# Hybrid decoder block on one core: 48 sums of 128x512 in the front moved from VectorE to accumulating DMAs of GpSimd's queue

## The chip, the core and the metric

The kernel runs on one core of a Trainium2 chip, as one launch. The metric is the device time in microseconds (us); several executions are given by their median. PE is the matmul engine (TensorE), DVE is VectorE, ACT is ScalarE, POOL is GpSimd, and SP is the engine whose queue issues nearly all loads and stores. Each engine works through its own instructions in the order in which they stand, and waits on semaphores for the others. A DMA is issued by an engine's queue and moved by 16 DMA engines that all queues share.

## The reference

One decoder layer on 1024 tokens of width 1024, in float32. Cut to what matters here:

```python
h = rmsnorm(x, norm_mix_pre)
q, k, v, gate, u = split(h @ w_in)                     # 4 heads of 128; u is 512 wide
qh, kh = rope(q), rope(k) * 128 ** -0.5                # x1*cos - x2*sin, x1*sin + x2*cos
y_ret = silu(gate) * groupnorm(retention(qh, kh, v))   # chunks of 128 tokens
# state space: 32 groups of 16 channels, 64 complex states each
states = scan(lam_bar, b_bar @ u)                      # s[t] = lam_bar*s[t-1] + bu[t]
y_ssm = glu(gelu(real(c @ states) + d * u))
x = x + rmsnorm(concat(y_ret, y_ssm) @ w_out, norm_mix_post)
x = x + rmsnorm(relu(rmsnorm(x) @ w_ff1) ** 2 @ w_ff2, norm_mlp_post)
```

## The kernel before

Tiles lie with 128 channels on the partitions and 512 tokens (or 128x4) in the free direction. Every large matmul is done as three passes over a high and a low part of its operands, which ACT and DVE make from each loaded tile (helper `split`, lines 133 to 139). The program runs in this order on PE: the projection to u, then gate, query and key projections (tiles pg and pj), the values (v), the gated unit (gl), the output projection (mx), and the two MLP products (f1, f2). The **front** is what stands ahead of mx.

Beside the projections, the front carries two side works on the same engines. One is the rotation of queries and keys: for each of 4 heads, query and key, and two halves of the tokens, `qk_unit` multiplies the projection by cosines (tile ra) and, with its halves exchanged, by sines (rb), and adds the two: 16 sums. The other is the state-space scan, which is cut into 8 **parts** of four channel groups (`ssm_part`, parts 0 to 7). The scan runs over 128 blocks of 8 tokens. A part has these steps:

- two products of small tables with phase factors, W and VV (`outer`: two products and a sum each). W makes, through the matmuls kps and wps, the tables MR and WT; VV is the table that turns states into outputs.
- the matmuls xps, which give 128 inputs of the scan; DVE rotates them by a phase (A = xps\*Fr, B = exchanged halves of xps times Fi, then A = A + B).
- four scans of DVE (line 529, B from A), the rotation back (A, C, then SS = A - C).
- the matmuls yps, which add the contribution of the tokens' own block (UT with MT) and that of the states (SS with VV); ACT takes the result (Y), and it is stored.

So a part has four sums of 128x512: W, VV, A and SS. In 8 parts these are 32, and with the rotation's 16 they are 48. A and SS of a part follow one another: SS needs the scans, the scans need A. The last four yps matmuls of a part are the only readers of SS.

The phase tables Fr and Fi come from tables fa and fb that POOL makes by a chain of small products (lines 312 to 317, then 433 and 434). POOL also clears each part's MR (line 506), and raises small tiles to the power -1/2 for the norms (lines 223 and 644). The norm of the first tokens needs such a power, and its result goes through PE again (nb_x, line 247).

The order on each engine is set when the program is built: a scheduler simulates the program with costs of its own and places each instruction where its operands are ready in that simulation. A change of an operation's engine therefore also moves other instructions.

Of the kernel before, what the change touches and what calls it, by code (L numbers as in the profile page):

```python
# [20 lines left out]
MUL, ADD, SUB = ALU.mult, ALU.add, ALU.subtract  # L21
# [3 lines left out]
P = 128  # L25
# [25 lines left out]
def hybrid_block_kernel(ctx, tc, x, xrow, gain, wu, wv, wqkg, wglu, wout, wff1, wff2, lam, bc, dsk,  # L51
                        rope, dmask, xi, zeta, sgn, edge, out):
    nc = tc.nc
    V, S, GP, TE = nc.vector, nc.scalar, nc.gpsimd, nc.tensor
# [8 lines left out]
    def half(name, dt=F32, shape=(P, 512)):  # L63
        tag = re.sub("[0-9_]+", "", name)
        return u2.tile(list(shape), dt, tag=tag, name=name, bufs=BUFS.get(tag))
# [4 lines left out]
    def mi_ps(name, shape=(P, 512)):  # L70
        return pm.tile(list(shape), F32, tag="mi", name=name)
# [22 lines left out]
    def ring(tag, shape, bufs):  # L94

        if tag not in rings:
            rings[tag] = [[const(f"{tag}{i}", shape) for i in range(bufs)], 0]
        r = rings[tag]
        r[1] += 1
        return r[0][r[1] % bufs]  # L100
# [13 lines left out]
    def load(dst, src, lead=None):  # L114
        r = nc.sync.dma_start(dst, src)
        if lead is not None:
            i = bisect.bisect_right(marks, clock[0] - lead, key=lambda m: m[0]) - 1
            if i >= 0:
                tc.add_manual_dep(r.ins, marks[i][1].name, gate_info, reason="load no earlier")
# [8 lines left out]
    def after_mark(r):  # L128
        if mark[0] is not None:
            tc.add_manual_dep(r.ins, mark[0].name, gate_info, reason="in order")  # L130
        return r

    def split(hi, lo, src, scale=None):
        if scale is None:
            after_mark(S.activation(hi, src, AF.Copy))  # L135
            V.tensor_tensor(lo, src, hi.bitcast(F32), op=SUB)  # L136
        else:
            S.activation(hi, src, AF.Copy, scale=scale)
            V.scalar_tensor_tensor(lo, src, scale, hi.bitcast(F32), op0=MUL, op1=SUB)
# [305 lines left out]
    s3 = (P, 4, P)  # L445
# [4 lines left out]
    def phase_tables(j):  # L450

        gs = slice(4 * j, 4 * j + 4)
        shf = [P, 4, T, 16]

        def lowp(m):
            return m[:, :, gs].rearrange("p a g -> p g a").unsqueeze(2).to_broadcast(shf)

        def highp(m):
            return m[:, :, gs].rearrange("p a g -> p g a").unsqueeze(3).to_broadcast(shf)

        def v4(m):
            return m.rearrange("p g (b a) -> p g b a", a=16)

        even, odd = ([half(f"F{z}{2 * j + i}", shape=s3) for z in "ri"] for i in range(2))
        tr, ti = half(f"ftr{j}", shape=s3), half(f"fti{j}", shape=s3)
        cmul(V, V, v4(even[0]), v4(even[1]), lowp(fa_r), lowp(fa_i), highp(fbr), highp(fbi),
             v4(tr), v4(ti))
        for e, o in zip(even, odd):
            load(o[0:64], e[64:128])
            load(o[64:128], e[64:128])  # L470
            load(e[64:128], e[0:64])
        phases[2 * j], phases[2 * j + 1] = even, odd

    def ssm_part(ei):
        if ei % 2 == 0:
            phase_tables(ei // 2)
        g0 = ei * 4
        gs = slice(g0, g0 + 4)
        UT = half(f"UT{ei}", shape=s3)
        for m in range(T):  # L480
            load(UT[m * GC:(m + 1) * GC],
                 ud[T - 1 - m, ei * 64:(ei + 1) * 64, :].rearrange("(g c) n -> c g n", c=GC))

        def outer(dst, a, lr, b, li, nm):
            tmp = half(f"tmp{nm}{ei}", shape=s4)

            def bx(m):
                return m[:, gs].unsqueeze(2).to_broadcast(list(s4))

            def by(m):  # L490
                return m[:, :, gs].rearrange("p m g -> p g m").unsqueeze(3).to_broadcast(list(s4))

            V.tensor_tensor(dst, bx(a), by(lr), op=MUL)
            V.tensor_tensor(tmp, bx(b), by(li), op=MUL)
            V.tensor_tensor(dst, dst, tmp, op=ADD)

        W = half(f"W{ei}", shape=s4)
        outer(W, a_b, qr, b_b, qi, "w")
        kt = ring("kt", (P, 4, GC), 2)
        kps = mi_ps(f"kps{ei}", (P, 4, GC))  # L500
        for g in range(4):
            TE.matmul(kps[:, g], W[:, g], cs[:, g0 + g], start=True, stop=True)
        S.activation(kt, kps, AF.Copy)
        V.tensor_tensor(kt[0:GC], kt[0:GC], de[0:GC, gs], op=ADD)
        MR = half(f"MR{ei}", shape=(P, T, 4, GC))
        GP.memset(MR, 0.0)
        for t in range(T):
            r0 = (T - 1 - t) * GC
            load(MR[r0:P, t], kt[0:P - r0])
        WT = half(f"WT{ei}", shape=s3)  # L510
        wps = mi_ps(f"wps{ei}", s3)
        for g in range(4):
            TE.transpose(wps[:, g], W[:, g].rearrange("p m c -> p (m c)"), ident)
        S.activation(WT, wps, AF.Copy)
        VV = half(f"VV{ei}", shape=s4)
        outer(VV, a_c, vr, b_c, vi, "v")
        yield
        Fr, Fi = phases.pop(ei)
        A, B = half(f"A{ei}", shape=s3), half(f"B{ei}", shape=s3)
        xps = mi_ps(f"xps{ei}", s3)  # L520
        for g in range(4):
            TE.matmul(xps[:, g], WT[:, g], UT[:, g], start=True, stop=True)
        V.tensor_tensor(A, xps, Fr, op=MUL)
        V.tensor_tensor(B[0:64], xps[64:128], Fi[64:128], op=MUL)
        V.scalar_tensor_tensor(B[64:128], xps[0:64], -1.0, Fi[0:64], op0=MUL, op1=MUL)
        V.tensor_tensor(A, A, B, op=ADD)
        yield
        for g in range(4):
            V.tensor_tensor_scan(B[:, g], rho[:, g0 + g:g0 + g + 1].to_broadcast([P, P]),
                                 A[:, g], 0.0, op0=MUL, op1=ADD)  # L530
        n1 = P - 1
        V.tensor_tensor(A[:, :, 0:n1], B[:, :, 0:n1], Fr[:, :, 0:n1], op=MUL)
        C = half(f"C{ei}", shape=s3)
        V.tensor_tensor(C[0:64, :, 0:n1], B[64:128, :, 0:n1], Fi[64:128, :, 0:n1], op=MUL)
        V.scalar_tensor_tensor(C[64:128, :, 0:n1], B[0:64, :, 0:n1], -1.0, Fi[0:64, :, 0:n1],
                               op0=MUL, op1=MUL)
        SS = half(f"SS{ei}", shape=s3)
        V.memset(SS[:, :, 0], 0.0)
        V.tensor_tensor(SS[:, :, 1:P], A[:, :, 0:n1], C[:, :, 0:n1], op=SUB)
        MT = half(f"MT{ei}", shape=s4)  # L540
        S.activation(MT.rearrange("p g t c -> p t g c"), MR, AF.Copy)
        yps = mi_ps(f"yps{ei}", s3)
        for g in range(4):
            TE.matmul(yps[:, g], MT[:, g], UT[:, g], start=True, stop=False)
            TE.matmul(yps[:, g], VV[:, g], SS[:, g], start=False, stop=True)
        Y = half(f"Y{ei}", shape=s3)
        S.activation(Y, yps, AF.Gelu_apprx_tanh)
        load(yd[:, :, gs, :].rearrange("t c g n -> (t c) g n"), Y)
        yield

    def ssm():
        parts = [ssm_part(ei) for ei in range(8)]
        yield next(parts[0])
        for ei in range(8):
            if ei < 7:
                yield next(parts[ei + 1])
            yield from parts[ei]
# [42 lines left out]
    def proj(name, w, hf):  # L600
        ps = acc_ps(name)
        for k in range(KB):
            mm3(ps, wblk(w, k), hT[k][hf], k == 0, k == KB - 1)
        return ps
# [57 lines left out]
    def tick():  # L662
        ticks[0] += 1
        step(1)
        pstep(1)
# [13 lines left out]
    def qk_unit(h, j, w):  # L679
        pair = []  # L680
        for hf in range(2):
            nm = f"{h}{j}{hf}"
            tick()
            ps = proj(f"pj{nm}", w, hf)
            a, b = half(f"ra{nm}", shape=s3), half(f"rb{nm}")
            af = a.rearrange("p c i -> p (c i)")
            V.tensor_tensor(af, ps, tabs[0][hf], op=MUL)
            S.activation(b[0:64], ps[64:128], AF.Copy)
            S.activation(b[64:128], ps[0:64], AF.Copy)
            V.tensor_tensor(b, b, tabs[1][hf], op=MUL)  # L690
            V.tensor_tensor(af, af, b, op=ADD)
            pair.append(a)
        qkv[h, j] = pair

# [131 lines left out]
    def comb(a, b, op, name=None):  # L826

        o = a if name is None else half(name)
        after_mark(V.tensor_tensor(o, a, b, op=op))  # L829
        return o  # L830
# [205 lines left out]
    for i in range(NP):  # L1036
# [3 lines left out]
        s3 = comb(a11, a21, SUB)  # L1040
# [100 lines left out]
    for i in range(NP):  # L1141
# [5 lines left out]
        else:  # L1147
            for b in range(4):
                a, t = ins[i]
# [4 lines left out]
    for c0 in (0, 256):  # L1154
        cols = slice(c0, c0 + 256)
        for b in range(4):
            around(b)
            if c0:
                for i in range(NP - NL, NP):
                    a, t = ins[i]  # L1160
# [103 lines left out]
```

## Time and profile before

| | |
|---|---|
| median of 3 runs | 1077.44 us (1076.61 to 1077.88) |
| the profiled execution, its own time | 1077.59 us |
| its span, first to last instruction | 1075.5 us |
| outside the span | 2.1 us |
| PE busy | 1049.9 us of the span (98%) |
| DVE busy | 770.1 us (72%) |
| ACT busy | 492.6 us (46%) |
| POOL busy | 68.8 us (6%) |
| mean granted clock of PE | 0.992 of full speed |

The profile is of one execution. The span is what the trace covers; the time of the execution is longer by 2.1 us. Times in the rows count from the span's start. Busy time of PE is the time in which some matmul is in flight, and matmuls overlap.

### The profile page before, as it was taken

The page shows a single profiled execution, that of the slowest core. Times are in us where ns is not written, and L with a number is a line of the kernel's source. Part 1 is how long each engine was busy: PE and PEld are TensorE (multiplying, and loading weights), DVE is VectorE, ACT ScalarE, POOL GpSimd, SP SyncE. Part 2 cuts the span into 40 slices and gives each one's busy share as a digit, 9 for nine tenths or more (in the row PEclk, how much of TensorE's full clock was granted, in tenths as well). Part 3 has the DMA queues.
Part 4 walks back from the last instruction along what each step waited for, and adds up shares of the span by engine and source line. Part 5 has one row for each costly group of instructions (what it writes and reads, how often), then busy time and mean ns, then how long its engine had stood idle before and what let it go on. Part 6 is the DMA issues. An engine that isn't in the chain of part 4 may idle for free.

```text
span 1075.5 us, 15286 instructions
## 1 busy us (share of the span) xinstructions
PE 1049.9 (98%) x5248; PEld 891.5 (83%) x5248; DVE 770.1 (72%) x1446; ACT 492.6 (46%) x916; POOL 68.8 (6%) x101
## 2 busy tenths in 40 slices
PE   7998999999999999999999999999999999999995
PEld 6877889989988888788888888888888888888895
DVE  7887999568766107478888888886763885756965
ACT  7332334355555224466644444464732553525712
POOL 0240000001000122300000000000000000000002
PEclk9998999999999999999999999999999999999998
DMA  9644343221431105386366666656982565579324
GB/s 317 205 125 114 98 123 96 74 79 36 133 103 58 41 1 200 115 309 229 126 228 234 231 237 224 214 183 218 375 276 85 181 203 175 187 229 328 127 85 150
DMA packets 126285, 181.58 MB, mean 169 GB/s; under 512 B 35584, under 2 KB 43776, under 8 KB 126208
## 3 DMA queue, kind: packets, MB, share of 16 engines
q1 hardware_dynamic: 125664, 180.09, 50.9%
q8 instruction: 41, 0.67, 0.2%
q10 hardware_dynamic: 544, 0.52, 0.1%
q14 instruction: 36, 0.29, 0.1%
HBM read 130.62 MB, written 45.61 MB: 164 GB/s over the span
## 4 chain that ended last, share of the span: by engine, by line
PE 79%; DVE 2%; issue 1%; DMA 1%; POOL 1%; ACT 1%; DVEq 0%; SPq 0%; ACTq 0%; POOLq 0%
PE f2x L106 15%; PE f2y L106 12%; PE f1z L106 8%; PE f1y L106 8%; PE mx L106 8%; PE f1x L106 8%; PE pj L106 4%; PE gl L106 4%; PE f1w L106 4%; PE v L106 3%; PE y L636 1%; PE st L611 1%; DMA raw_wo<-wout_dram 1%; PE y L638 1%; PE sps L622 1%
## 5 line engine op out<-in xcount | busy, mean ns | idle before, releaser
L106 PE MATMUL f2x<-hi_tc,lo_sb 128*128 128x512 f32 x216 | 84.0, 389 | 0.0
L106 PE MATMUL f2x<-lo_tc,hi_sb 128*128 128x512 f32 x216 | 84.0, 389 | 0.0
L106 PE MATMUL f2x<-hi_tc,hi_sb 128*128 128x512 f32 x216 | 83.7, 390 | 0.0
L135 ACT ACTIVATE hi_sa<-rawa 128x512 fp32r<-128x512 f32 x80 | 48.3, 622 | 59.2 <-DVE rawa L829 57.0
L106 PE MATMUL f2y<-hi_tc,hi_sb 128*128 128x512 f32 x192 | 74.7, 389 | 0.0
L106 PE MATMUL f2y<-lo_tc,hi_sb 128*128 128x512 f32 x192 | 74.7, 389 | 0.0
L106 PE MATMUL f2y<-hi_tc,lo_sb 128*128 128x512 f32 x192 | 74.7, 389 | 0.0
L136 DVE TENSOR_TENSOR lo_sa<-rawa,hi_sa 128x512 fp32r<-128x512 f32 x80 | 56.3, 710 | 8.9 <-ACT hi_sa L135 8.9
L223 POOL TENSOR_TENSOR small<-small 128x4 f32<-128x4 f32 (+1 forms) x9 | 10.1, 1119 | 653.1 <-DVE small L221 653.1
L106 PE MATMUL pj<-hi_h,hi_wqkg 128*128 128x512 f32 x128 | 50.8, 397 | 0.0
L106 PE MATMUL pj<-lo_h,hi_wqkg 128*128 128x512 f32 x128 | 50.7, 396 | 0.0
L106 PE MATMUL pj<-hi_h,lo_wqkg 128*128 128x512 f32 x128 | 50.5, 395 | 0.0
L106 PE MATMUL f1x<-lo_tb,hi_sa 128*128 128x512 f32 x128 | 49.9, 390 | 0.4 <-DVE lo_tb L136 0.4
L106 PE MATMUL f1x<-hi_tb,hi_sa 128*128 128x512 f32 x128 | 50.1, 392 | 0.0
L106 PE MATMUL f1y<-hi_tb,hi_sa 128*128 128x512 f32 x128 | 49.8, 389 | 0.0
L106 PE MATMUL f1y<-lo_tb,hi_sa 128*128 128x512 f32 x128 | 49.8, 389 | 0.0
L106 PE MATMUL f1y<-hi_tb,lo_sa 128*128 128x512 f32 x128 | 49.8, 389 | 0.0
L106 PE MATMUL f1z<-hi_tb,hi_sa 128*128 128x512 f32 x128 | 49.8, 389 | 0.0
L106 PE MATMUL f1z<-lo_tb,hi_sa 128*128 128x512 f32 x128 | 49.8, 389 | 0.0
L106 PE MATMUL f1z<-hi_tb,lo_sa 128*128 128x512 f32 x128 | 49.8, 389 | 0.0
L106 PE MATMUL f1x<-hi_tb,lo_sa 128*128 128x512 f32 x128 | 49.3, 390 | 0.0
L106 PEld LDWEIGHTS f2x<-lo_tc,hi_sb 128*128 128x128 f32 x216 | 40.6, 188 | 8.4
(398 smaller groups left out, 2998.9 us busy)
## 6 DMA issues: line engine op xcount, KB each, us to landing
rawa<-wff_dram SPq DMA_DIRECT2D x92, 256.0 KB, 3.3
tinx<-td SPq DMA_DIRECT2D x48, 256.0 KB, 3.9
tiny<-td SPq DMA_DIRECT2D x48, 256.0 KB, 3.4
raw_wqkg<-wqkg_dram SPq DMA_DIRECT2D x24, 256.0 KB, 2.9
x<-x_dram SPq DMA_DIRECT2D x16, 256.0 KB, 5.4
xt<-xrow_dram SPq DMA_DIRECT2D x16, 256.0 KB, 3.7
raw_wo<-wout_dram SPq DMA_DIRECT2D x16, 256.0 KB, 3.4
xr<-x_dram SPq DMA_DIRECT2D x16, 256.0 KB, 3.4
```

Source lines behind the costliest of these rows:

```text
L106: r = TE.matmul(out_, lhsT, rhs, **kw)
L135: after_mark(S.activation(hi, src, AF.Copy))
L136: V.tensor_tensor(lo, src, hi.bitcast(F32), op=SUB)
L223: GP.tensor_tensor(r, t, mhalf[:, 0:n], op=ALU.pow)
L611: TE.matmul(stp[:, i], k_[:, i], q_[:, i], start=True, stop=True)
L622: TE.matmul(sps[:, i], kz[:, i], v_[:, i], start=True, stop=True)
L636: TE.matmul(yps[:, i], smk[:, i], v_[:, i], start=True, stop=(c == 0))
L638: TE.matmul(yps[:, i], q_[:, i], Rs[(c - 1) // 4][:, (c - 1) % 4], start=False, stop=True)
```

## The change

A new helper issues an accumulating DMA from GpSimd's queue: it reads the source tile and the destination tile, and writes their sum to the destination. All 48 sums named above go through it. For SS, whose second term was subtracted, the signs of C's two products are exchanged, and the products are written at their shifted place at once, with the first column of both tiles cleared; so the sum can cover the whole tile. That adds one DVE memset for each part. The new lines shift the line numbers behind them by 4: line 529 is line 533 after the change.

```diff
+    def dma_add(o, a):
+
+        GP.dma_start(o, a, accum_op=ADD)
+
...
             V.tensor_tensor(dst, bx(a), by(lr), op=MUL)
             V.tensor_tensor(tmp, bx(b), by(li), op=MUL)
-            V.tensor_tensor(dst, dst, tmp, op=ADD)
+            dma_add(dst, tmp)
...
         V.scalar_tensor_tensor(B[64:128], xps[0:64], -1.0, Fi[0:64], op0=MUL, op1=MUL)
-        V.tensor_tensor(A, A, B, op=ADD)
+        dma_add(A, B)
         yield
...
         n1 = P - 1
-        V.tensor_tensor(A[:, :, 0:n1], B[:, :, 0:n1], Fr[:, :, 0:n1], op=MUL)
-        C = half(f"C{ei}", shape=s3)
-        V.tensor_tensor(C[0:64, :, 0:n1], B[64:128, :, 0:n1], Fi[64:128, :, 0:n1], op=MUL)
-        V.scalar_tensor_tensor(C[64:128, :, 0:n1], B[0:64, :, 0:n1], -1.0, Fi[0:64, :, 0:n1],
+        SS, C = half(f"SS{ei}", shape=s3), half(f"C{ei}", shape=s3)
+        V.memset(SS[:, :, 0], 0.0)
+        V.memset(C[:, :, 0], 0.0)
+        V.tensor_tensor(SS[:, :, 1:P], B[:, :, 0:n1], Fr[:, :, 0:n1], op=MUL)
+        V.scalar_tensor_tensor(C[0:64, :, 1:P], B[64:128, :, 0:n1], -1.0, Fi[64:128, :, 0:n1],
                                op0=MUL, op1=MUL)
-        SS = half(f"SS{ei}", shape=s3)
-        V.memset(SS[:, :, 0], 0.0)
-        V.tensor_tensor(SS[:, :, 1:P], A[:, :, 0:n1], C[:, :, 0:n1], op=SUB)
+        V.tensor_tensor(C[64:128, :, 1:P], B[0:64, :, 0:n1], Fi[0:64, :, 0:n1], op=MUL)
+        dma_add(SS, C)
...
             V.tensor_tensor(b, b, tabs[1][hf], op=MUL)
-            V.tensor_tensor(af, af, b, op=ADD)
+            dma_add(af, b)
```

The order of instructions on three engines, at the places that the prediction speaks of. The digit behind a tile's name is the part, and the number behind it is the buffer's.

DVE, from the rotation of part 0's scan inputs to its SS. Before:

```order
L526 TENSOR_TENSOR A0_952<-A0_952,B0_953 128x512
L673 TENSOR_TENSOR ga30_1254<-pg30_1229,R0_398 128x512
L529 SCALAR_TENSOR_TENSOR B0_953<-small_72,A0_952 128x128 x4
L675 SCALAR_TENSOR_TENSOR ga30_1254<-gb30_1255,ga30_1254 128x512
L532 TENSOR_TENSOR A0_952<-B0_953,Fr0_776 128x4x127
L534 TENSOR_TENSOR C0_998<-B0_953,Fi0_777 64x4x127
L535 SCALAR_TENSOR_TENSOR C0_998<-B0_953,Fi0_777 64x4x127
L136 TENSOR_TENSOR lo_wqkg1_0_1335<-raw_wqkg1_0_1332,hi_wqkg1_0_1334 128x512
L493 TENSOR_TENSOR W3_1268<-bc0_276,qw_608 128x512
L539 TENSOR_TENSOR SS0_1001<-A0_952,C0_998 128x4x127
```

After:

```order
L529 SCALAR_TENSOR_TENSOR B0_953<-xps0_954,Fi0_777 64x512
L508 TENSOR_TENSOR small_72<-small_72,de_732 16x64
L677 TENSOR_TENSOR ga30_1256<-pg30_1231,R0_398 128x512
L533 SCALAR_TENSOR_TENSOR B0_953<-small_72,A0_952 128x128 x4
L679 SCALAR_TENSOR_TENSOR ga30_1256<-gb30_1257,ga30_1256 128x512
L539 TENSOR_TENSOR SS0_997<-B0_953,Fr0_776 128x4x127
L540 SCALAR_TENSOR_TENSOR C0_998<-B0_953,Fi0_777 64x4x127
L542 TENSOR_TENSOR C0_998<-B0_953,Fi0_777 64x4x127
```

The two sums are gone from DVE. The scans now wait for the DMA of A, and between B and the scans stand two other instructions, a short one and one of 128x512.

POOL, from the end of the chain for fb to the power that the second half's norm needs. Before:

```order
L314 TENSOR_TENSOR fb_668<-fb_668,t8_610 128x16
L317 TENSOR_TENSOR fb_668<-fb_668,t8_610 128x16
L506 MEMSET MR2_1099 128x512
L223 TENSOR_TENSOR small_72<-small_72 128x4
L506 MEMSET MR3_1280 128x512
```

After:

```order
L318 TENSOR_TENSOR fb_668<-fb_668,t8_610 128x16
L321 TENSOR_TENSOR fb_668<-fb_668,t8_610 128x16
L510 MEMSET MR2_1100 128x512
L135 DMA W2_1088<-tmpw2_1089 128x512
L227 TENSOR_TENSOR small_72<-small_72 128x4
L135 DMA A0_952<-B0_953 128x512
L135 DMA SS0_997<-C0_998 128x512
L135 DMA W3_1270<-tmpw3_1271 128x512
L135 DMA A1_1152<-B1_1153 128x512
L510 MEMSET MR3_1282 128x512
L135 DMA VV2_1117<-tmpv2_1118 128x512
L135 DMA SS1_1209<-C1_1210 128x512
```

The DMAs of all parts stand in one queue with the memsets and the powers. Ahead of this piece, three DMAs (VV0, W0, VV1) stand in front of the chain for fa and one (W1) inside the chain for fb.

PE, where the xps matmuls of part 4 stand. Before:

```order
L106 MATMUL pj110_1759<-hi_h70_174,hi_wqkg4_1_1600 128x512
L522 MATMUL xps4_1750<-UT4_1474,WT4_1505 128x128 x4
L106 MATMUL pj110_1759<-lo_h70_175,hi_wqkg4_1_1600 128x512
L106 MATMUL pj110_1759<-hi_h70_174,lo_wqkg4_1_1601 128x512
L106 MATMUL pj111_1816<-hi_h01_204,hi_wqkg4_0_1594 128x512
```

After:

```order
L548 MATMUL yps3_1621<-UT3_1261,MT3_1619 128x128
L549 MATMUL yps3_1621<-SS3_1611,VV3_1299 128x128
L526 MATMUL xps4_1754<-UT4_1477,WT4_1508 128x128 x4
L106 MATMUL pj110_1763<-hi_h00_84,hi_wqkg4_0_1597 128x512
L106 MATMUL pj110_1763<-lo_h00_85,hi_wqkg4_0_1597 128x512
```

Before, the xps matmuls of part 4 stood ahead of the yps matmuls of part 3 that read SS; after, they stand right behind them. Counted over the whole front, the matmuls between the last xps and the first yps that reads SS, for parts 0 to 7, were 60, 78, 87, 111, 136, 69, 108 and 82 before (of 512 columns: 47, 62, 74, 91, 26, 50, 0 and 0), and are 70, 82, 73, 71, 80, 69, 114 and 109 after (of 512 columns: 57, 66, 60, 55, 48, 50, 0 and 0; nearly all others of parts 4, 6 and 7 have 256 columns).

## Rows read from the trace of the kernel before

**Rows 1.** The page, part 1: busy us (share of the span) and instructions of each engine.

```profile
PE 1049.9 (98%) x5248; PEld 891.5 (83%) x5248; DVE 770.1 (72%) x1446; ACT 492.6 (46%) x916; POOL 68.8 (6%) x101
```

**Rows 2.** Idle time of PE by what ended it: us in total, times, longest.

```profile
PE u L106 <- ACT hi_h L138: 5.9, 1, 5.9
PE nb_x L247 <- POOL small L223: 5.8, 1, 5.8
PE yps L545 <- DVE SS L539: 1.4, 1, 1.4
```

**Rows 3.** Three stretches of the front: us, busy time by engine, clock, DMA share, GB/s.

```profile
75.00:100.00 25.00, 19.14 (x77) 15.37 (x76) 19.66 (x32) 7.91 (x14) 2.02 (x1) 0.86 0.43 114
100.00:175.00 75.00, 75.00 (x429) 65.42 (x429) 72.88 (x127) 26.97 (x47) 2.11 (x4) 1.00 0.38 106
175.00:345.00 170.00, 168.49 (x1110) 153.15 (x1109) 121.76 (x278) 82.37 (x165) 11.31 (x9) 1.00 0.28 81
```

**Rows 4.** Timeline, 64 to 87 us: start, duration, instruction, idle time ahead of it.

```profile
64.06 1.06 DVE L312 TENSOR_TENSOR Fr<-fa,fb 128x512 f32<-128x512 f32 x1 [4.12 <-POOL fb L314]
...
82.27 0.15 DVE L221 TENSOR_SCALAR small<-small 128x4 f32<-128x4 f32 x1
...
82.50 2.02 POOL L223 TENSOR_TENSOR small<-small 128x4 f32<-128x4 f32 x1 [14.88 <-DVE small L221]
...
84.57 2.07 PE L247 MATMUL nb_x<-small 128*128 128x128 f32 x8 [5.77 <-POOL small L223]
...
86.87 0.63 PE L106 MATMUL pg<-hi_h,lo_wqkg 128*128 128x512 f32 x1
```

**Rows 5.** DVE's groups, 0 to 320 us: count | busy us, mean ns of one.

```profile
L691 DVE TENSOR_TENSOR ra<-ra,rb 128x512 f32<-128x512 f32 x16 | 11.0, 687 | 0.2
...
L526 DVE TENSOR_TENSOR A<-A,B 128x512 f32<-128x512 f32 x8 | 5.5, 683 | 0.0
```

**Rows 6.** The longest pieces of the chain that ended last, 60 to 345 us: start, us.

```profile
201.22 5.25 PE pj L106 x23
...
281.93 7.66 PE v L106 x64
```

**Rows 7.** Timeline of part 0 (first two), part 4 and part 7 (last four).

```profile
101.87 1.05 PE L522 MATMUL xps<-UT,WT 128*128 128x128 f32 x8
...
102.96 0.69 DVE L523 TENSOR_TENSOR A<-xps,Fr 128x512 f32<-128x512 f32 x1 [1.54 <-PE xps L522]
...
161.31 1.05 PE L522 MATMUL xps<-UT,WT 128*128 128x128 f32 x8
...
168.62 0.67 DVE L523 TENSOR_TENSOR A<-xps,Fr 128x512 f32<-128x512 f32 x1
...
182.95 0.68 DVE L539 TENSOR_TENSOR SS<-A,C 128x508 f32<-128x508 f32 x1
...
183.69 0.49 PE L545 MATMUL yps<-SS,VV 128*128 128x128 f32 x2 [1.37 <-DVE SS L539]
...
278.21 1.06 PE L522 MATMUL xps<-UT,WT 128*128 128x128 f32 x8
...
281.62 0.68 DVE L523 TENSOR_TENSOR A<-xps,Fr 128x512 f32<-128x512 f32 x1
...
288.66 0.69 DVE L539 TENSOR_TENSOR SS<-A,C 128x508 f32<-128x508 f32 x1
...
289.43 0.47 PE L545 MATMUL yps<-SS,VV 128*128 128x128 f32 x2
```

**Rows 8.** DMA issues: count, KB each, median us from issue to landing.

```profile
ud<-uT SPq DMA_DIRECT2D x8, 256.0 KB, 2.6
...
yd<-Y SPq DMA_DIRECT2D x8, 256.0 KB, 2.1
...
MR<-small SPq DMA_DIRECT2D x8, 32.0 KB, 1.9
```

**Rows 9.** POOL's groups: count | busy us, mean ns of one.

```profile
L644 POOL TENSOR_TENSOR small<-small 128x4 f32<-128x4 f32 x8 | 10.8, 1349 | 143.2 <-DVE small L643 143.2
...
L506 POOL MEMSET MR<- 128x512 f32 x8 | 4.2, 527 | 102.3 <-DMA Fi<-Fi 51.3 <-DMA Fr<-Fr 21.3 <-DMA MR<-small 16.9
```

**Rows 10.** POOL's timeline, 57 to 61 us: two products of one size.

```profile
57.63 2.26 POOL L313 TENSOR_TENSOR t<-fb 128x16 f32<-128x16 f32 x1
...
60.04 0.21 POOL L316 TENSOR_TENSOR t<-fb 128x16 f32<-128x16 f32 x1
```

**Rows 11.** Instructions of two lines: count, ns min/median/max, first and last start.

```profile
L691 DVE TENSOR_TENSOR ra<-ra,rb x16: 670/686/698, 130.9 to 272.0; 128x512 f32<-128x512 f32 x16
...
L611 PE MATMUL st<-ra,ra x64: 270/275/275, 197.4 to 322.2; 128*128 128x128 f32 x64
```

## The prediction

> **What bounds the kernel now.** I read the busy times first: PE is busy in 98% of the span, DVE in 72%, POOL in 6% [rows 1]. So DVE's average says nothing; what counts is where PE stands still. The list of PE's waits answers that: 5.9 us at the start, 5.8 us before nb_x, 1.4 us before one yps, and nothing else worth a term in the front [rows 2]. The stretches show the same [rows 3]: between 100 and 175 us PE has no gap, although DVE is busy for 72.9 of 75 us there. Freed DVE time is therefore worth nothing by itself. What the change can win is at most those two waits.
>
> The 5.8 us are worth looking at. PE waits from 78.8 us for nb_x, which waits for POOL's power (2.02 us), which waits for a DVE instruction at 82.27 us that is queued behind the making of Fr and Fi, begun at 64.06 us when POOL's chain for fb ended [rows 4]. Behind the wait PE runs at the lower clock for a while: 0.86 of full speed over that stretch [rows 3].
>
> **What leaves.** 16 sums of the rotation take 11.0 us of DVE and A's eight 5.5 us [rows 5]; the eight each of W, VV and SS take about as much as A's. That is 33 us of busy time, off PE's path. Of part 4, SS was the wait of 1.4 us [rows 2, 7]. The eight new memsets, and the exchanged signs, cost DVE well under 1 us and are hidden in its idle time.
>
> **What comes: the price of one accumulating DMA.** Call T the time from the moment that its operands are ready and POOL issues it to the landing. No row shows such a DMA, and none a DMA of POOL's queue. Bounds: a plain DMA of 256 KB issued by SP takes 2.1 to 2.6 us [rows 8], and an accumulating one can't do less; I take 2.6 as the low end, since ud is written in the busy part of the front. Upwards, it also reads its destination, and POOL has to issue it. From 32 KB to 256 KB the landing grows by 0.7 us [rows 8], so one more stream of 256 KB may cost 0.8; a whole second DMA would cost 2.6. POOL's issue may cost between its memset (0.53) and its power of four elements (1.35) [rows 9]. So T lies between 2.6 and 2.6 + 2.6 + 1.35 = 6.5 us, and I take 2.6 + 0.8 + 0.8 = **4.2 us**, where a DVE sum took 0.69.
>
> The Trainium skill (DMA: Bandwidth & Descriptors, Anatomy of one DMA, the gpsimd path) gives about 2.0 us and the bytes at 436 GB/s for one DMA of GpSimd's queue, an estimate of 2.6 us for 256 KB; it says nothing there of accumulation. By it alone T would be at the low end, and the time that of the rival "hidden" below.
>
> **Where T is hidden.** The rotation's sums began at 130.9 us at the earliest and their first reader, st, at 197.4; the last ones are 272.0 and 322.2 [rows 11]. Tens of microseconds cover them, and VV is read even later after its sum. W feeds kps sooner, but W1's DMA can go before the point where DVE formerly got to its sum. I cost these 32 sums at nothing; without cover, a part's kps would wait for T less a sum's 0.69, 3.5 us.
>
> **Where T is not hidden.** In each part, A and SS lie in series between xps and yps, and PE is in order. For one part
>
> wait of PE = L + F + 2T - D.
>
> F is what the chain takes apart from its two sums. The leanest case is part 7: from A at 281.62 to the end of SS at 289.35 us [rows 7] are 7.73, less two sums of 0.69: F = 6.35. L is how late DVE comes to A after xps. In part 0 it comes at once, in part 4 6.3 us late (168.62 against 162.36), in part 7 2.4 us late [rows 7]; read so for the eight parts, L is 0, 2.9, 4.7, 7.8, 6.3, 0.7, 0.9, 2.4. D is PE's work between xps and the first yps that reads SS, in the new order. A matmul of 512 columns takes 0.228 us and one of 256 takes 0.120 [rows 6], a small one about 0.2; with the counts of the order D is 15.3, 18.0, 16.0, 15.5, 14.8, 15.2, 15.0 and 14.0 us. The order moved against the change here: parts 2, 3 and 4 had 19.2, 24.6 and 20.0 us before. In the piece shown, xps of part 4 has slid behind yps of part 3, so a late SS of one part also delays the inputs of the next.
>
> At T = 4.2, L + 14.75 - D gives 0, 0, 3.4, 7.0, 6.2, 0.2, 0.6 and 3.1: together 20.5 us. Less the old wait of 1.4: 19.1. L should shrink a little. Between 100 and 175 us 22 sums leave DVE, 13 us at 0.6 apart; but DVE now stands at each scan until A has landed, with only 0.7 to 3 us of other work placed in between, some 2 to 3.5 us for a part, which takes back most of it. I take 1 us off each of parts 2, 3, 4 and 7: **+15 us**.
>
> The wait before nb_x I leave as it is. DVE's queue between Fr and that instruction loses one sum (W2, 0.6 us) and some sums ahead of it; but one DMA (W1) now stands inside POOL's chain for fb and W2's ahead of the power, at 0.53 to 1.35 each by the bounds above, and nb_x itself stands five matmuls (1.1 us) earlier on PE. From mx on nothing changes and PE is gapless there but for the waits of the end, so what the front loses is lost. The profiled execution took 1077.59 us for a span of 1075.5, 0.15 above the median of the runs: 1077.6 + 15 = **1093 us**.
>
> **The rivals.**
>
> *Hidden.* With T at 2.6, L + 11.55 - D is above 0.3 in parts 3 and 4 alone (3.8 and 3.0), and there DVE, standing at the scans for 1 us or less, gains enough (13 us in five parts) to come to A that much sooner. Then only the old 1.4 us leave: 1076 us, no difference that can be told. For it: plain DMAs land in 2.1 to 2.6. Against: the second stream and POOL's issue come on top. It turns at T of about 3. Chance 0.14.
>
> *The wait before nb_x goes.* This ends on the other side, faster. If DVE, with four sums fewer by 80 us, reached the short instruction before the power some 4 us sooner, PE would not stop at 78.8 us and the clock not fall: 5.8 us. The clock of 0.86 over 25 us is 7 us at half speed [rows 3], some 5 of them behind the wait, worth about 2.5 us. With the 1.4 of yps this is 1068 us, with T hidden. For it: that wait is the largest in the front. Against: Fr's start hangs on POOL's chain, DVE already sat idle for 4.12 us before it [rows 4], and POOL has more to do there, not less. It takes a POOL issue well below 0.5 us. Chance 0.06.
>
> *POOL's queue becomes the bound.* All 48 DMAs, the memsets and the powers stand in one queue in order. POOL is slow beside a busy DVE: a product that takes 0.21 us took 2.26 while DVE ran one two-input product after another [rows 10]. If an issue takes 2 us and T is 6.5, L + 19.35 - D is above zero in all parts: 57 us, less 1.4: about 1133; W1 and the powers for the head norms come late as well. Chance 0.15.
> The Trainium skill (DMA: Bandwidth & Descriptors, SWDGE vs HWDGE vs iDMA) has a rule that speaks for this one: GpSimd writes the descriptors of its DMAs into SBUF itself, and VectorE's two-port modes lock it out. The slow product above is of POOL's own reads; whether the writing of descriptors suffers here no row shows.
>
> **How the numbers follow.** My forecast, T between 3 and 5.6, has 0.65. At T = 5.6 the formula gives L + 17.55 - D, together 42, less 4 for L and 1.4: 1115 us. Hidden 0.14, nb_x 0.06, POOL 0.15. The range of 1076 to 1116 holds the forecast and the hidden case and leaves out nb_x and most of POOL's, about 0.2. It is wide because the slope is: up to 16 us for each microsecond of T once all eight parts wait. A measurement of this kernel tells 0.2% (2.2 us) from no change: slower 0.80 (forecast and POOL), same 0.13 (most of hidden), faster 0.07.
>
> **What would show it right or wrong.** In the changed profile PE's waits should name yps waiting for the DMA of SS, 1 to 7 us in five or six parts, longest in parts 3 and 4, together 15 to 22 us; DVE should sit idle before the scans for A's DMA. The DMA list gives T at once. DVE's busy time should fall by about 33 us, and the stretch from mx on should be as long as before. No wait before kps, st or ktp. I am wrong if T is under 3 (then no yps waits), if POOL shows issues of 2 us (then kps and the powers wait too), or if nb_x no longer waits.

## The result, and the profile after

The changed kernel takes 1101.44 us (median of 4 runs, 1100.66 to 1102.99), the kernel before 1077.06 us in the same comparison (4 runs): a ratio of 1.0225, 95% interval 1.0214 to 1.0237. It is 24.4 us slower; the forecast was 15.6 us slower than the median of before, with a range up to 1116 us. The profiled execution has a span of 1099.6 us, 24.1 more than before; the ledger below is made on the spans.

Busy time by engine (the page, part 1), as in [rows 1]:

```profile
PE 1055.5 (96%) x5248; PEld 894.9 (81%) x5248; DVE 744.6 (68%) x1406; ACT 492.2 (45%) x916; POOL 106.6 (10%) x149
```

Idle time of PE by what ended it, us in total, times, longest, as in [rows 2]:

```profile
PE yps L549 <- DMA SS<-C: 11.8, 5, 4.3
PE u L106 <- ACT hi_h L142: 5.9, 1, 5.9
PE nb_x L251 <- POOL small L227: 4.3, 1, 4.3
PE yps L549 <- DVE ra L691: 4.2, 1, 4.2
PE yps L549 <- issue: 1.7, 1, 1.7
PE kps L506 <- DMA W<-tmpw: 1.6, 1, 1.6
PE yps L549 <- DVE C L538: 1.4, 1, 1.4
```

DVE lost 25.5 us of busy time and gained nothing by it. PE now stands before the first yps matmul that reads SS in every part: 11.8 + 4.2 + 1.7 + 1.4 = 19.1 us, where it was 1.4. Only five of the eight waits are put down to the DMA of SS. In the other three the timeline has the same DMA: in part 4 SS's DMA is issued at 184.77 us, PE goes on at 188.65, and the "ra" named is a DVE product that merely ended last before it (at 187.96 us). A releaser's name is a guess where several things end together.

Three stretches of the front, as in [rows 3] (us, busy time of PE, PEld, DVE, ACT, POOL, clock, DMA share, GB/s):

```profile
75.00:100.00 25.00, 20.74 (x86) 17.02 (x85) 19.10 (x30) 6.85 (x13) 1.42 (x1) 0.86 0.45 115
100.00:175.00 75.00, 66.27 (x357) 56.71 (x356) 57.52 (x106) 24.17 (x43) 20.08 (x25) 0.95 0.78 169
175.00:345.00 170.00, 159.49 (x1054) 145.45 (x1053) 96.47 (x220) 70.92 (x143) 26.48 (x30) 0.98 0.48 116
```

Between 100 and 175 us PE had no gap before; it now has 8.7 us of gaps, at a clock of 0.95. DVE came down from 72.9 to 57.5 us there, and the DMA engines' share went from 0.38 to 0.78. The first mx matmul starts at 374.5 us instead of 351.8: 22.7 of the 24.1 us are lost in the front. Ahead of mx PE's idle time grew from 13.2 to 31.0 us and its busy time by 4.9 us.

DMA issues, as in [rows 8] (count, KB each, median us from issue to landing):

```profile
ra<-rb POOLq DMA_DIRECT2D x16, 256.0 KB, 4.0
VV<-tmpv POOLq DMA_DIRECT2D x8, 256.0 KB, 4.6
W<-tmpw POOLq DMA_DIRECT2D x8, 256.0 KB, 4.5
ud<-uT SPq DMA_DIRECT2D x8, 256.0 KB, 3.1
UT<-ud SPq DMA_DIRECT2D x64, 32.0 KB, 2.5
A<-B POOLq DMA_DIRECT2D x8, 256.0 KB, 3.9
SS<-C POOLq DMA_DIRECT2D x8, 256.0 KB, 4.5
```

T was forecast at 4.2 us, and A and SS stand at 3.9 and 4.5. The fit that gives an estimate of 2.6 us for 256 KB (the Trainium skill, DMA: Bandwidth & Descriptors, Anatomy of one DMA) does not hold for these accumulating DMAs: the measurement decides. POOL's groups say what an issue costs POOL, as in [rows 9] (count | busy us, mean ns | idle before, with its releasers):

```profile
L135 POOL DMA_DIRECT2D SS<-C x8 | 7.2, 894 | 31.4 <-DVE C L542 23.6 <-PE v L106 6.5 <-DVE SS L539 1.2
L135 POOL DMA_DIRECT2D A<-B x8 | 6.9, 867 | 39.2 <-DVE small L508 21.3 <-ACT hi_wo L139 7.4 <-DVE B L529 4.2
```

It is 0.87 to 0.89 us, not 2, and POOL is idle ahead of most of them: it waits for operands, so its queue is not the bound. The timeline of part 1 shows one chain as a whole (start, duration, instruction, idle time ahead of it):

```profile
106.89 1.06 PE L526 MATMUL xps<-UT,WT 128*128 128x128 f32 x8
111.93 0.68 DVE L527 TENSOR_TENSOR A<-xps,Fr 128x512 f32<-128x512 f32 x1
114.94 0.85 POOL L135 DMA_DIRECT2D A<-B  x1 [1.60 <-DVE B L529]
...
117.04 0.39 PE L549 MATMUL yps<-SS,VV 128*128 128x128 f32 x2
117.49 0.39 PE L549 MATMUL yps<-SS,VV 128*128 128x128 f32 x2
...
121.07 1.37 DVE L533 TENSOR_TENSOR_SCAN B<-small,A 128x128 f32<-128x128 f32 x4 [0.86 <-DMA A<-B]
126.42 1.13 POOL L135 DMA_DIRECT2D SS<-C  x1
130.80 0.77 PE L549 MATMUL yps<-SS,VV 128*128 128x128 f32 x2 [4.32 <-DMA SS<-C]
131.79 0.63 PE L549 MATMUL yps<-SS,VV 128*128 128x128 f32 x2
132.64 0.64 PE L549 MATMUL yps<-SS,VV 128*128 128x128 f32 x2
```

A is 4.0 us late after xps, A's DMA takes 6.1 us until the scan starts, SS's 4.4, and PE waits 4.3. Behind the wait the matmuls are slow: 0.63 us each and 0.85 apart, where those of the part before, some 14 us earlier, took 0.39 and stood 0.45 apart. The clock of that stretch says why (PE alone: us, busy time, clock, DMA share, GB/s):

```profile
121.00:126.00 5.00, 5.00 (x31) 1.00 0.38 116
130.80:135.40 4.60, 4.60 (x21) 0.50 0.50 90
188.65:193.40 4.75, 4.75 (x22) 0.50 0.76 160
```

The granted clock is 0.50 there, the lower level of 1.2 GHz. It fell so at the two longest yps waits, of part 1 and part 4. PE was busy at the lower clock for 4.6 and 4.75 us, which is work for half as long: 4.7 us lost, nearly all of the 4.9 us by which its busy time ahead of mx grew. Before, the front had one such place, behind nb_x, and it still has it.

### The profile page after: what moved, and what is told of

The parts are those of the page before. It is cut to its first block, busy times and chain, and to the rows that moved or that the text cites. A ratio compares the mean times of both kernels' runs of the same rounds, so it can differ in the third digit from the quotient of the medians.

```text
span 1099.6 us, 15384 instructions
## 1 busy us (share of the span) xinstructions
PE 1055.5 (96%) x5248; PEld 894.9 (81%) x5248; DVE 744.6 (68%) x1406; ACT 492.2 (45%) x916; POOL 106.6 (10%) x149
## 4 chain that ended last, share of the span: by engine, by line
PE 79%; DMA 6%; DVE 6%; issue 4%; POOL 2%; ACT 1%; SPq 1%; DVEq 0%; ACTq 0%; POOLq 0%
PE f2x L106 15%; PE f2y L106 12%; PE f1z L106 8%; PE f1y L106 8%; PE f1x L106 7%; PE mx L106 6%; PE f1w L106 4%; PE v L106 4%; PE gl L106 4%; PE pj L106 3%; PE u L106 3%; DMA A<-B 2%; PE pg L106 1%; SPq L115 1%; DMA xt<-xrow_dram 1%
```

## The experiments

Twelve kernels were run. The table orders them by what they vary: which sums are DMAs, and whose order PE follows. "Own" is the order that the scheduler made for that kernel; the other two hold PE to the order of the kernel before or of the changed one. The last column is the ratio to the kernel before, times 1077, less 1077.

| run | by DMA | PE's order | median us | ratio to before (95%) | us |
|---|---|---|---|---|---|
| changed kernel | all 48 | own | 1101.44 | 1.0225 (1.0214 to 1.0237) | +24.2 |
| e1_scan_by_dma | A, SS | own | 1093.15 | 1.0132 (1.0113 to 1.0151) | +14.2 |
| e2_rest_by_dma | W, VV, ra | own | 1089.99 | 1.0102 (1.0085 to 1.0119) | +11.0 |
| e6_yps_later | all 48, yps later | own | 1109.39 | 1.0287 (1.0268 to 1.0306) | +30.9 |
| e8_extra_dmas | none, 48 extra | own | 1106.93 | 1.0268 (1.0250 to 1.0286) | +28.9 |
| x0_none_order_before | none | before's | 1079.63 | 1.0015 (1.0006 to 1.0023) | +1.6 |
| x4_rest_order_before | W, VV, ra | before's | 1083.41 | 1.0051 (1.0039 to 1.0063) | +5.5 |
| x2_dma_order_before | all 48 | before's | 1107.95 | 1.0272 (1.0258 to 1.0286) | +29.3 |
| x3_extra_order_before | none, 48 extra | before's | 1102.22 | 1.0222 (1.0208 to 1.0236) | +23.9 |
| x6_load_order_before | none, 48 plain extra | before's | 1085.33 | 1.0068 (1.0056 to 1.0080) | +7.3 |
| x1_none_order_after | none | changed's | 1089.78 | 1.0106 (1.0092 to 1.0120) | +11.4 |
| x7_rest_order_after | W, VV, ra | changed's | 1084.79 | 1.0068 (1.0056 to 1.0080) | +7.3 |
| y2_early_order_before | W1, W2, VV0, VV1 | before's | 1078.32 | 1.0000 (0.9991 to 1.0009) | 0.0 |

### One half of the change at a time

The theory was that the two DMAs in series make the loss; the rivals were the load of 48 DMAs, and that the other 32 were costed too low. In e1 the helper is called for A and SS alone:

```diff
-            dma_add(dst, tmp)
+            V.tensor_tensor(dst, dst, tmp, op=ADD)
...
-            dma_add(af, b)
+            V.tensor_tensor(af, af, b, op=ADD)
```

> Only the 16 sums A and SS go by accumulating DMA; the 32 sums W, VV and ra are DVE's again. Theory (two DMAs in series between xps and yps, each some 4.2 us from issue to landing, and a half clock behind the longer waits): with PE's work between xps and yps in this kernel's order (15.6, 17.2, 19.5, 19.3, 17.8, 15.6, 16.6, 14.8 us) and the late starts L of the kernel before, the waits of yps are 0, 0.5, 0, 3.3, 3.3, 0, 0, 2.4 us, together 9.3; less the old 1.4, with up to 4 us for the clock, 1085 to 1089 us. Rival (the load of 48 DMAs on GpSimd's queue and the DMA engines): a third of the DMAs is left, a third of the loss, about 1085 us, but then without waits of yps for SS of more than 2 us and with landings shorter than 4 us.

Measured: +14.2 us, more than either expected. The yps waits are those of the theory in kind, 11.6 us in five parts, but the longest is of part 6 (5.6 us), where none was expected. In e2 it is the other way round:

```diff
-        dma_add(A, B)
+        V.tensor_tensor(A, A, B, op=ADD)
...
-        dma_add(SS, C)
+        V.tensor_tensor(SS, SS, C, op=ADD)
```

> Only the 32 sums W, VV and ra go by accumulating DMA; A and SS are DVE's, in the changed form of SS. Theory (only the series of A and SS costs): no yps waits, 1077 us, or down to 1074 us where the old yps wait of 1.4 us and a part of the wait before nb_x go too. Rival (load on GpSimd's queue and the DMA engines): two thirds of the DMAs are left and two thirds of the loss, about 1093 us. Rival (32 sums were costed too low, kps or st wait): waits of kps or st by name, 1 to 3.5 us for each part.

Measured: +11.0 us, 1090 us: nearest to the 1093 of the load. Of the waits by which the last rival was to show, there is one, of 1.5 us, before kps. PE's idle time of this kernel names another cause:

```profile
PE yps L549 <- DVE SS L543: 7.6, 2, 5.7
...
PE yps L548 <- ACT Y L551: 2.4, 1, 2.4
PE kps L506 <- DMA W<-tmpw: 1.5, 1, 1.5
```

There is no DMA in A or SS, and yet yps waits 7.6 us for DVE's SS. The scheduler, whose DVE has 32 sums less here, has put yps closer behind xps: 12.7 us of work between them in part 4, where the kernel before has 20.0 counted in the same way, while DVE comes to A of that part 8.0 us after the end of xps (169.09 against 161.05). So the order is a suspect of its own, and a run with another order does not show what a DMA costs.

### Two runs that did not tell what they were built to tell

> All 48 sums by accumulating DMA as in the changed kernel; only the yps matmuls stand later on PE, behind 10 to 45 more projection matmuls for a part. Theory: the same DMAs with the same landings of 3.9 to 4.6 us, but no yps wait of more than 0.3 us, perhaps one of part 7; the half-speed stretches behind them go as well: 1075 to 1078 us, with the wait before nb_x still there. Rival (load): the DMAs and their load are unchanged, so 1095 to 1101 us, with the waits at other places.

```diff
+            r = TE.matmul(yps[:, g], VV[:, g], SS[:, g], start=False, stop=True)
+            tc.add_manual_dep(r.ins, marks[min(YPS_AT[ei], len(marks)) - 1][1].name, gate_info,
+                              reason="in order")
```

YPS_AT is a list of one place for each part, and the yps steps are issued later in the program. Measured: +30.9 us. The yps waits did fall, from 19.1 to 4.6 us (all in part 7). But v then waited 4.8 us for hi_wvb, gl 2.6, pj 2.3, nb_x 6.6, and PE's busy time grew to 1063.5 us. The later yps moved the rest of the order with them; this run settles nothing about the DMAs.

> The kernel before with all its sums on DVE, and 48 accumulating DMAs of 128x512 more on GpSimd's queue, which read the same tiles and add them into four tiles that nothing reads. Theory: nothing waits for them, so 1077 to 1080 us; the powers for nb_x may stand behind an issue of 0.86 us. Rival (load on the queue, the DMA engines and SBUF): the whole loss shows here too, 1095 to 1101 us, with late weights or late tables of a part.

```diff
+            junk.extend(half(f"junk{i}") for i in range(4))
...
+        GP.dma_start(junk[0], a, accum_op=ADD)
```

Measured: +28.9 us, more even than the rival had, but at least in part by a flaw of the experiment: in the kernel before, A is written anew behind the scans, and so DVE had to wait until the extra DMA had read it (DVE's A behind "junk", 7.8 us in four waits).

### The order and the DMAs taken apart

The next kernels hold PE to a recorded order, so that only what runs in it differs:

```diff
+    seq = [i for s, n in PE_ORDER for i in range(s, s + n)]
+    for u, v in zip(seq, seq[1:]):
+        tc.add_manual_dep(pes[v], pes[u].name, gate_info, reason="in order")
```

PE_ORDER is the list of PE's instructions in the order of the kernel before or of the changed one, from its 308th to its 1684th; the two orders are equal outside of these. The dependence orders the program and is no wait on the chip. Only PE is held: DVE, ACT, POOL and SP are still ordered by the scheduler. In these kernels all matmuls carry the line of one helper (L80 or L81).

> All 48 sums on DVE, SS in its changed form (signs exchanged, two memsets), and PE held to the order of its instructions in the kernel before. Both theories: 1077 to 1079 us; the changed form and the holding of the order cost nothing. If it is slower than 1081 us, the form or the holding has a price that the other runs of this set have to be read against.

Measured: +1.6 us, the price of holding and of the changed form of SS together. The one yps wait is 1.8 us here (1.4 before), and behind it the granted clock fell, which it had not before (PE alone, columns as above):

```profile
185.00:188.00 3.00, 3.00 (x16) 0.50 0.59 159
```

> All 48 sums on DVE, but PE held to the order of its instructions in the changed kernel. Theory (the landing of the DMAs makes yps wait): with a sum of 0.69 in place of 4.2 us, L + 7.75 - D is below zero in all parts, so no yps wait of note, 1076 to 1079 us. Rival (the order that the scheduler made, with less work between xps and yps in parts 2 to 4, and side steps placed as if DVE were freer, is what costs): half of the loss or more is here too, 1089 us or more.

Measured: +11.4 us with no sum as a DMA, so the order does cost. PE's idle time in x1:

```profile
PE nb_x L80 <- POOL small L261: 7.9, 1, 7.9
PE yps L80 <- DVE SS L577: 6.0, 3, 2.6
```

The waits of yps are in parts 2, 3 and 4, those whose work between xps and yps shrank in the changed order. SS is ready 18.6, 22.6 and 15.7 us behind xps there, against 17.6, 23.5 and 21.3 before.

> All 48 sums by accumulating DMA as in the changed kernel, but PE held to the order of the kernel before. Theory: with that order's work between xps and yps (13.1, 17.2, 19.2, 24.6, 19.4, 15.1, 13.8, 9.4 us) the waits of yps by L + 14.75 - D are 1.7, 0.5, 0.3, 0, 1.7, 0.4, 1.9 and 7.8, together 14 us, longest in part 7; with one or two half-speed stretches 1090 to 1095 us. Rival (the order alone): near 1077 us. Rival (the load of the DMAs): 1095 to 1101 us, with waits for weights, tables or powers by name and not for SS.

Measured: +29.3 us, more than any of the three had, and worse than with the changed order. So the changed order is not simply bad: for slow sums it is better than the old one, for fast sums worse. In x2 the longest yps waits are 7.2 us in part 6 and 5.3 in part 7, where the old order has little work to put between, and 4.7 us went to MT. ACT makes one of them at 162.82 us (150.47 before), right behind its copies to rb, ahead of which it stood idle for 9.81 and 4.89 us. The second of these ended with DVE's scans, which had waited for A's DMA:

```profile
161.60 0.59 ACT L727 ACTIVATE rb<-pj 64x512 f32<-64x512 f32 x1 [4.89 <-DVE B L568]
...
162.82 0.63 ACT L580 ACTIVATE MT<-MR 128x512 f32<-128x512 f32 x1
```

> The changed kernel with A and SS alone put back on DVE: the other 32 sums stay DMAs, and PE is held to the order of the changed kernel. Theory (the series of A's and SS's DMAs makes the yps waits): L + 7.75 - D is below zero in all parts, so the yps waits and the half-speed stretches behind them go: 1078 to 1084 us. Rival (the order of the changed kernel costs by itself): about 1090 us, as with all sums on DVE in that order. Rival (load): 1093 us or more.

```diff
-        dma_add(A, B)
+        V.tensor_tensor(A, A, B, op=ADD)
...
-        dma_add(SS, C)
+        V.tensor_tensor(SS, SS, C, op=ADD)
```

This is the run that decides: PE's order is that of the changed kernel, 32 sums are still DMAs, and only the two in series are gone. Measured: +7.3 us instead of +24.2. PE's idle time in x7:

```profile
PE nb_x L80 <- POOL small L261: 4.2, 1, 4.2
PE yps L80 <- DVE SS L577: 3.1, 2, 2.1
PE yt L86 <- ACT yn L686: 3.0, 2, 2.3
PE kps L80 <- DMA W<-tmpw: 1.4, 1, 1.4
```

Sixteen of the 48 DMAs thus cost 24.2 - 7.3 = 16.9 us in this order. With the order of before they cost 29.3 - 5.5 = 23.8 us (x2 against x4). What yps had waited for was 19.1 us; not all comes back, since yps then waits 3.1 us for DVE, and yt 3.0 us. The four waits shown are 4.5 us more than those of yps and nb_x before. The half-speed stretches did not all go either: the granted clock was 0.50 from 178 to 180 us and from 280 to 283, behind waits of 2.1 us (yps) and 2.3 (yt). So the time, 1084.8 us, lies 0.8 above the theory's range.

### Are the other 32, and the load as such, free?

> The 32 sums W, VV and ra by accumulating DMA, A and SS on DVE, and PE held to the order of the kernel before. Theory (these 32 are hidden; what the same 32 cost with the scheduler's own order came from the order): 1077 to 1081 us, with the yps wait of 1 to 2 us at most. Rival (the load of the DMAs on GpSimd's queue and the DMA engines, or POOL's other work queued behind them): 1088 us or more, with waits for tables MT, for W or for weights by name.

Measured: +5.5 us, of which 1.6 are the control's: about 4 us for 32 DMAs in the order of before, between the theory and its rival. PE's idle time in x4:

```profile
PE xps L81 <- DMA UT<-ud: 5.3, 1, 5.3
PE nb_x L81 <- POOL small L262: 3.6, 1, 3.6
PE kps L81 <- DMA W<-tmpw: 1.5, 1, 1.5
```

On PE no reader waits for VV or ra. W is waited for once, and one part's scan inputs come late: UT's loads are issued from 159.56 us (154.94 before). On SP they stand behind the same part's loads of MR, which go out from 151.15 us (143.22 before). SP's order is another here, and ahead of these loads it stood still until a DMA of ra had landed, though the load it held back (raw_wvb, at 148.60 us) doesn't read ra:

```profile
SPq L150 <- DMA ra<-rb: 2.5, 1, 2.5
```

> All 48 sums on DVE and PE held to the order of the kernel before, as in the first of this set, with 48 accumulating DMAs of 128x512 more on GpSimd's queue: each is issued when the sum it stands for is done (behind a copy of one element of it) and adds one tile that is never written again into one of four others that nothing reads, so no other work waits for its data. Theory: as the first of this set, within 3 us (a power may stand behind an issue of 0.86 us). Rival (load of the queue and of the DMA engines): 1090 us or more, with late weights, tables or powers.

Measured: +23.9 us. Again an added dependence spoils it: a DMA into one of four spare tiles waits on POOL until an earlier one into the same tile has landed (POOL waits 15.3 us for that, in six waits), and xps waits 6.5 us for UT, v 6.3 us and yps 4.6 us for DVE; what each of these hangs on was not followed. The last of this kind has a place in DRAM for each DMA:

```diff
+        t = GP.tensor_copy(go, o[0:1, 0:1])
+        r = GP.dma_start(spare[n_spare[0]], src)
+        tc.add_manual_dep(r.ins, t.ins.name, gate_info, reason="in order")
```

> All 48 sums on DVE and PE held to the order of the kernel before. 48 plain DMAs of 256 KB on GpSimd's queue are added, each from one tile that is never written again to a place in DRAM of its own, issued when the sum that it stands for is done (behind a copy of one element), so that none waits for another's data as in the earlier run of this kind. Theory: 1079 to 1083 us. Rival (load): 1090 us or more, with inputs of xps, tables or weights late.

Measured: +7.3 us, 5.7 above the control, so the load is not free, but it is far from 24. (It is not quite the same load: these DMAs don't read their destination, and the 48 copies on POOL come on top.) PE's idle time in x6, and its added DMAs:

```profile
PE nb_x L81 <- POOL small L270: 5.9, 1, 5.9
PE pg L81 <- DVE lo_wqkg L183: 2.6, 1, 2.6
PE xps L81 <- DMA UT<-ud: 2.2, 1, 2.2
```

```profile
spare<-src POOLq DMA_DIRECT2D x48, 256.0 KB, 2.9
```

A weight and UT come late, behind a shift of SP's queue (UT is issued from 161.26 us, 154.94 before) or on busier DMA engines; which of the two was not separated.

### A version meant to beat both

> The kernel before with 4 of the 48 sums alone by accumulating DMA, those of W1, W2, VV0 and VV1, which stand ahead of the wait for nb_x and are read at least 10 us later; PE is held to the order of the kernel before, W0 (for which kps waited 1.4 to 2.0 us) stays on DVE. In the runs with W and VV by DMA that wait was 3.6 to 4.3 us, in those without 5.8. Theory (DVE comes sooner to the short instruction ahead of the power): the wait for nb_x is 3.6 to 4.3 us and nothing else is new, 1075 to 1076.5 us, the only version so far below the kernel before. Rival (the wait hangs on POOL's chain and on the order, not on these sums): 5.8 us as before and 1077 to 1079 us.

```diff
+            if nm + str(ei) in ("v0", "v1", "w1", "w2"):
+                GP.dma_start(dst, tmp, accum_op=ADD)
+            else:
+                V.tensor_tensor(dst, dst, tmp, op=ADD)
```

Measured: 1078.32 us, a ratio of 1.0000 (0.9991 to 1.0009). PE's idle time in y2:

```profile
PE kps L81 <- DMA W<-tmpw: 3.6, 1, 3.6
PE nb_x L81 <- POOL small L258: 3.2, 1, 3.2
```

The wait before nb_x did shrink, by 2.6 us; another wait took its place. The expectation was wrong about the readers: a W is read by kps at once. W1's DMA stood in POOL's chain for fb and was issued at 58.19 us, and PE went on at 62.59. Nor does the wait for nb_x shrink whenever W and VV go by DMA: in e6 it was 6.6 us. No version tried is faster than the kernel before.

## Why the prediction was right, and where it fell short

**What bounds the kernel.** Right. DVE's busy time fell by 25.5 us (33 were forecast; in the timeline independent instructions of 0.69 stand 0.60 apart, so a sum of 0.69 frees less than that), and the time rose.

**T.** Right: 3.9 and 4.5 us for A and SS, where 4.2 was taken, the "hidden" case needed 2.6 and POOL's rival 6.5. POOL's issue was taken at 0.8 and is 0.87 to 0.89 in these.

**The wait of yps.** The mechanism was right and the sum near: 20.5 - 4 = 16.5 us with the old wait, against 19.1. That it came so near is in part luck: by part the forecast, with 1 us off in parts 2, 3, 4 and 7, is off by 1.6 us on average and by 4.3 in part 1, and two of its terms were off in opposite directions. From the timeline, read for each part as in part 1:

| part | 0 | 1 | 2 | 3 | 4 | 5 | 6 | 7 |
|---|---|---|---|---|---|---|---|---|
| L taken | 0 | 2.9 | 4.7 | 7.8 | 6.3 | 0.7 | 0.9 | 2.4 |
| L after | 0 | 4.0 | 0 | 5.4 | 5.0 | 0 | 1.6 | 4.0 |
| A's DMA issued to scan | 3.7 | 6.1 | 5.6 | 4.2 | 3.8 | 4.9 | 3.3 | 3.4 |
| SS's DMA issued to yps | 4.9 | 4.4 | 5.8 | 3.8 | 3.9 | 3.7 | 5.0 | 5.0 |
| wait forecast (T = 4.2) | 0 | 0 | 3.4 | 7.0 | 6.2 | 0.2 | 0.6 | 3.1 |
| wait measured | 0.2 | 4.3 | 2.1 | 2.1 | 4.2 | 1.4 | 1.7 | 3.1 |

L shrank by 5.7 us over the eight parts, a little more than the 4 us allowed. DVE did stand before the scans, 1.9 us for a part:

```profile
L533 DVE TENSOR_TENSOR_SCAN B<-small,A 128x128 f32<-128x128 f32 x32 | 11.0, 406 | 15.2 <-DMA A<-B 15.2
```

F + 2T was 14.75; it measures 16.0 (the two DMA rows average 4.4 and 4.6, and the stretches from A's start to its DMA and from the scan to SS's DMA 2.7 and 4.4), so the parts taken as free or nearly so (0, 1, 5, 6) wait too. That the longest waits would be those of parts 3 and 4 held for part 4 alone. The formula took the eight waits as independent, and they are not: where xps of a part stands ahead of the last part's yps, the wait of that yps gives the next chain time. Read from the timeline, D is within 0.6 us of the forecast in six parts, but 18.0 in part 3 (15.5 taken), with part 2's wait of 2.1 in it, and 15.8 in part 7 (14.0 taken), with part 6's 1.7 in it. That the two DMAs in series are the main cause is shown by x7: 16.9 us come back when A and SS alone return to DVE.

**What the sum left out.** Three steps failed. The new stalls were priced at their length only; the lower clock behind two of them costs 4.7 us more. "No wait before kps": there is one, 1.6 us, since W1's DMA stands in POOL's chain and is issued at 56.09 us. And the 32 sums "at nothing": with A and SS on DVE again, 7.3 us remain in the changed order (x7), and about 4 in the old one (x4). The prediction looked at the readers of W, VV and ra, where all but W's were indeed covered; it did not ask what else waits for a DMA to land. In the changed kernel DVE waits 11.7 us in all before it writes tmpv and tmpw anew, which these DMAs read, and ACT 6.1 us before rb; how much of this reaches PE was not separated. Nor did it ask what the scheduler does with PE's order when DVE has fewer sums. With the wait before nb_x, left at 5.8 and now 4.3, the ledger of the span is 17.7 (yps) + 4.7 (clock) + 1.6 (kps) - 1.5 (nb_x) = 22.5 of 24.1 us. Of the other 1.6, 1.4 lie behind the start of mx; they are not assigned.

**The rivals.** "POOL's queue becomes the bound" is out by its price: no issue of the 48 took over 1.21 us, though DVE was busy for 57.5 of 75 us beside them. The rule of the Trainium skill that spoke for it (DMA: Bandwidth & Descriptors, SWDGE vs HWDGE vs iDMA) did not show here, and no row tells whether any instruction of DVE was in such a mode. A milder form is true: that queue's order delays W1. "The wait before nb_x goes" came in part (1.5 us), worth far less than the new waits.

**Still open.** How the 7.3 us of x7 divide between the 32 DMAs, SP's queue, and the order: x1 costs more in that order with no sum as a DMA, so the parts do not add up, and DVE's, POOL's and SP's own orders were not held.

## What to carry to other kernels

Move a sum to a DMA only where its reader is many times a landing away: what counts is the chain between two steps of the engine that bounds, and two landings in series at 8 places there cost 17 us in one order of PE and 24 in another, while 25.5 us of another engine's time came free for nothing. A far reader alone did not make the other 32 free: they left 4 to 7 us. Price each new stall with the clock behind it, and each DMA also by what waits for it to land without reading its result. Where a scheduler sets the order, hold the order before comparing halves of a change: with own orders the two halves cost 14.2 and 11.0 us, and in one held order 7.3 and, as the rest of the whole, 16.9.

## What was not expected of the hardware

- An accumulating DMA of 256 KB from SBUF to SBUF landed 3.9 to 4.6 us after its issue in the changed kernel (medians; 3.8 for the extra ones of x3, 5.0 for A's in x2), a plain one of the same queue and size from SBUF to DRAM in 2.9 us (x6). The destination differs too, so the difference of 0.9 us or more is not accumulation alone for certain.
- While the DMA share between 100 and 175 us doubled to 0.78, DMAs of SP's queue landed later as well: UT in 2.5 us (1.8 before), ud in 3.1 (2.6 before).
- In the changed kernel the clock fell at yps waits of 4.3 and 4.2 us and not at that of 3.1 us. The length of the wait alone doesn't tell: in x0 the granted clock was 0.50 behind a yps wait of 1.8 us, and in x7 behind waits of 2.1 and 2.3. What decides was not tested.
